# Three FFN blocks of a one-core decoder layer with six seven-product steps instead of five, another order of the low parts in runs of three, and the copies for premade weight sums on SyncE's queue

## The chip, the cores and the metric

One core of a Trainium2 chip runs one launch of the kernel. The metric is device time in microseconds (us), the median of three runs. The profile is one further execution of the same program.

## The reference

One trunk layer of a decoder, for 256 tokens, width 2048, all in float32. What matters here is how much of it is matrix products:

```
a = rmsnorm(h, norm_mix_pre);  proj = a @ w_in                     # 2048 x 17408
attn = three dilated-window attention groups;  r_out = gated linear recurrence (HGRN2)
y = sigmoid(gate_a) * (attn @ w_attn_branch) + sigmoid(gate_r) * (r_out @ w_hgrn_branch)
h = h + rmsnorm(y @ w_mix_out, norm_mix_post)                      # 2048 x 2048
a = rmsnorm(h, norm_ffn_pre)
gt, up = split(a @ w_ffn_gate_up)                                  # 2048 x 11264
h = h + rmsnorm((silu(gt) * up) @ w_ffn_down, norm_ffn_post)       # 5632 x 2048
```

The change lies in the product with `w_ffn_gate_up`.

## The kernel before

**High and low parts.** TensorE multiplies in a rounded float32 format. Each operand is therefore split: the high part is a rounded copy that ScalarE makes, the low part is what VectorE finds by subtracting the copy from the operand. A product is then three matmuls, high x high, high x low and low x high (`prod`, which calls `mm`, L171). For a weight tile of 128x2048 these parts are `w` (L399, ScalarE) and `wl` (L407, VectorE).

**Wide blocks and steps.** The gate and up columns are worked off in eleven blocks of 512 gate and 512 up columns. Block 0 is done in another way; blocks j = 1 to 10 are `Wide` blocks. Such a block has eight steps. A step takes two of the sixteen 128-row slices of the weights, for both column groups (gate, up) and both sides (the first and the last 128 tokens): a 2x2x2 product of tiles. Done plainly that is eight products, 24 matmuls. By Strassen and Winograd's scheme it is seven products, 21 matmuls, if sums are at hand: sums of activation tiles (`h7`, made once for each pair of slices by `pair_sums`, kept for all blocks) and three sums of weight tiles (`sum`, 128x1536, made for each step anew). These sums are split too: `dh` (L427, ScalarE) and `dl` (L430, VectorE). There is one buffer for `dh` and one for `dl`, so `dh` of one step can't be written before the last matmul that reads `dh` of the seven-product step before it.

**Which steps are by seven.** The strings of `FFN` tell it: "87877877" for j = 2 to 10 means that steps 1, 3, 4, 6 and 7 are by seven products. `order` gives the pairs of slices 0 to 4 to the sevens and 5 to 7 to the eights, so `h7` is needed for five pairs (`H7`).

**The order within a step.** In `multiply_wide` a seven-product step is a string of products. The letters o, u, 1 and 7 read `w` and `wl`; t, 6 and 5 read `dh` and `dl`. The letter x is the transposition of the finished block before, which is put into step 1. The order depends on the neighbours: "ou1x6t57" in step 1, "t65ou17" where a seven follows, "ou17t65" where one came before, "1765out" in a last step after a seven. After the last step `gather` takes the products 1, 6, 5 and 7 out of their banks (L534 on ScalarE, L536 to L539 on VectorE), and `add_up` adds the rest (L552).

**Premade sums.** Three VectorE additions make the sums of a step (`add_weights`, L415 to L417). For the steps in `READY` they are made long before by DMA in a DRAM tile: `sums_before` issues three copies (L458) and, some steps later, three accumulating DMAs (L462), all from GpSimd's queue (POOL). `get_ready` loads the result (L439, SyncE's queue, SP). In blocks 2 to 10 steps 1 and 3 have such sums; 4, 6 and 7 don't. `READY_IN` lists the units of the program in which `sums_before` goes a little further.

**What sets the order.** It is written out by hand. For each step n, `ahead(n)` issues what later steps need: the split of step n+2 (`split_wide`: high part, then its sums if they aren't premade, then the low part), the split of the sums of step n+1 (`split_sums`, in `st.rest`), and, in `load_behind`, the weight load that the freed buffer allows. Where steps n and n+1 are both by seven (`close`), the split of the sums is put off until the matmuls of step n are issued (`later`). Weight loads go through SP's queue; for a seven-product step an accumulating DMA from POOL's queue (L308) adds one slice to another in the loaded tile. Three `raw` buffers and a fourth hold loaded weights.

Of the kernel before, what the change touches and what calls it, by code (L numbers as in the profile page):

```python
# [32 lines left out]
COL_QR, COL_FR, COL_IR, COL_GR = 9216, 10240, 11264, 12288  # L33
COL_GA, COL_GB = 13312, 15360

X7, H7 = tuple(range(5)), tuple(range(5))
MIX = [[(3, 0), (4, 0), (5, 0), (0, 1), (6, 0), (1, 1), (2, 0), (7, 0)],
       [(3, 0), (4, 0), (0, 1), (5, 0), (1, 1), (2, 0), (6, 0), (7, 0)]]

# [4 lines left out]


EARLY = [order(x) for x in ["88878878", "87878787"] + ["87877877"] * 6 + ["88787787", "88787878"]]
FFN = [order(x) for x in ["88878787"] + ["87877877", "87877877", "87877877", "87877877", "87877877", "87877877", "87877877", "87877877", "87877877"]]
# [9 lines left out]
BESIDE, LAG = (2, 3, 4, 5, 6, 7), 22  # L57
WIDE_FQ, FLIP = 2, 1
KEPT_P, KEPT, KEPT_H = (18,), (6, 10), (16,)
READY, PACE, READY_IN, READY_TWICE = {(2, 1), (2, 3), (3, 1), (3, 3), (4, 1), (4, 3), (5, 1), (5, 3), (6, 1), (6, 3), (7, 1), (7, 3), (8, 1), (8, 3), (9, 1), (9, 3), (10, 1), (10, 3), (11, 6), (11, 10), (11, 14), (12, 4), (12, 8), (12, 12), (12, 16)}, (4, 6), ((-5, 0), (2, 110)), ((2, 64),)  # L60


class Block:
# [48 lines left out]
def tile_hybrid_block(ctx: ExitStack, tc: tile.TileContext, t, out):  # L112
    nc = tc.nc
# [333 lines left out]
    def sums_before(steps):  # L447

        def one(st):
            b = st.block  # L450
            m = b.order[st.i][0]
            t00, t01, t10, t11 = (
                b.w[(2 * m + k) * P : (2 * m + k + 1) * P, c : c + 512] for k in range(2) for c in b.cols
            )
            st.ready = dram.tile([P, 1536], F32, name=nm("ready"))
            mid, row, all4 = (st.ready[:, n * 512 : (n + 1) * 512] for n in range(3))
            for dst, src in (row, t00), (mid, t10), (all4, t11):
                nc.gpsimd.dma_start(dst, src)  # L458
            for dst, src in (row, t01), (mid, row), (all4, mid):
                for _ in range(PACE[0]):  # L460
                    yield
                nc.gpsimd.dma_start(dst, src, accum_op=OP.add)  # L462

        going = []
        while steps or going:
            if steps and (len(going) < 1 or all(g[1] >= PACE[1] for g in going)):
                going.append([one(steps.pop(0)), 0])
            for g in list(going):
                g[1] += 1
                if next(g[0], "end") == "end":  # L470
                    going.remove(g)
            yield

    def multiply_wide(st, sides=(0, 1), groups=(0, 1)):
# [1002 lines left out]
    def second_norm():  # L1477
        ss, s2 = small("ss"), small("s2")
        yield
        for n in range(8):  # L1480
            j, b = n // 2, n % 2
            nc.scalar.activation(
                ptile("junk"), h_t[j][:, b, :], AF.Square,
                accum_out=ss[:, 4 * b + j : 4 * b + j + 1],
            )
            if n < 4 or b == 1:
                yield
        add_parts(s2[:, :2], ss)
        rsqrt_mean(r2c, s2[:, :2], D)
        ready.add("r2")  # L1490
        if len(H7) > 4:
            for n in range(len(H7) - 2):
                kept["h", n] = dram.tile([P, 1024], F32, name=nm("kept"))
                nc.gpsimd.dma_start(kept["h", n], h_t[n].rearrange("p b c -> p (b c)"))

    def more_sums():
        for n in range(len(H7) - 2):
            h_t.pop(n)
        slot = lambda: hslot("so").rearrange("p b c -> p (b c)").bitcast(F32R)
        lanes[1].append(pair_sums(hT[0], H7[4:], h7, slot))  # L1500

    def h_back():
        for n in range(len(H7) - 2):
            h_t[n] = hslot("h")
            nc.gpsimd.dma_start(h_t[n].rearrange("p b c -> p (b c)"), kept["h", n])

# [281 lines left out]
    def ahead(n):  # L1788
# [22 lines left out]
        def rest():  # L1811
            next(parts, None)
# [17 lines left out]
    for n, st in enumerate(seq):  # L1830
# [118 lines left out]
```

## Time and profile before

| what | value |
|---|---|
| median of three runs | 1676.74 us (1676.22 to 1677.0) |
| the profiled execution's own time | 1675.0 us |
| its span, first to last instruction | 1673.2 us |
| granted TensorE clock, mean | 0.999 |
| busy: PE (matmul) / DVE (VectorE) / ACT (ScalarE) / POOL (GpSimd) | 1661.8 / 1477.7 / 960.5 / 230.4 us |
| matmuls | 8028 |
| chain that ended last | 93% PE, 3% DVE, 2% DMA |

Times in the profile are us from the span's start. PEld is TensorE's weight load, which overlaps the matmuls. A row of the timeline gives start, length, engine, source line, operation and `out<-in`; in brackets stands idle time just before and what ended it. Matmuls are pipelined, so a matmul that is shown with 0.39 us is followed by the next one earlier than that: the distance of the starts is what it costs.

The FFN blocks stand in the trace one behind the other, 41.1 us each: block 1 begins at about 1025 us, block 2 at 1066, block 4 at 1148, block 5 at 1189, block 10 at 1395; the down projection begins at 1436.

### The profile page before, as it was taken

The page shows a single profiled execution, that of the slowest core. Times are in us where ns is not written, and L with a number is a line of the kernel's source. Part 1 is how long each engine was busy: PE and PEld are TensorE (multiplying, and loading weights), DVE is VectorE, ACT ScalarE, POOL GpSimd, SP SyncE. Part 2 cuts the span into 40 slices and gives each one's busy share as a digit, 9 for nine tenths or more (in the row PEclk, how much of TensorE's full clock was granted, in tenths as well). Part 3 has the DMA queues.
Part 4 walks back from the last instruction along what each step waited for, and adds up shares of the span by engine and source line. Part 5 has one row for each costly group of instructions (what it writes and reads, how often), then busy time and mean ns, then how long its engine had stood idle before and what let it go on. Part 6 is the DMA issues. An engine that isn't in the chain of part 4 may idle for free.

```text
span 1673.2 us, 21505 instructions
## 1 busy us (share of the span) xinstructions
PE 1661.8 (99%) x8028; PEld 1390.4 (83%) x8028; DVE 1477.7 (88%) x1512; ACT 960.5 (57%) x959; POOL 230.4 (14%) x309
## 2 busy tenths in 40 slices
PE   9999999999999999999999999999999999999997
PEld 7888888888888888888888888888888888888886
DVE  6799999999987998867668888999999999899988
ACT  6566555565665444445445565666666666666664
POOL 0001111111003311313311010111111111000100
PEclk9999999999999999999999999999999999999999
DMA  8888888998769997969988857998988989887892
GB/s 283 268 261 258 269 244 264 277 289 274 234 204 316 313 268 219 279 209 303 297 249 250 279 187 245 274 277 273 282 280 268 283 268 278 255 256 236 258 307 103
DMA packets 235705, 436.56 MB, mean 261 GB/s; under 512 B 15408, under 2 KB 65632, under 8 KB 235600
## 3 DMA queue, kind: packets, MB, share of 16 engines
q1 hardware_dynamic: 195920, 345.94, 61.3%
q0 software_dynamic: 37056, 83.32, 22.7%
q10 hardware_dynamic: 2624, 5.92, 1.0%
q8 instruction: 63, 1.03, 0.3%
q14 instruction: 42, 0.34, 0.1%
HBM read 422.01 MB, written 52.43 MB: 284 GB/s over the span
## 4 chain that ended last, share of the span: by engine, by line
PE 93%; DVE 3%; DMA 2%; issue 1%; ACT 1%; SPq 0%; DVEq 0%; POOLq 0%; ACTq 0%
PE acc L171 52%; PE aux L171 39%; DMA raw<-in_w_mix_out 2%; DVE wl L407 1%; PE aux L1033 0%; DMA x<-in_x 0%; ACT w L399 0%; DVE dl L430 0%; PE acc L1534 0%; DVE fz L1666 0%; PE aux L651 0%; PE aux L1534 0%; DVE w L361 0%; ACT junk L1621 0%; ACT dh L427 0%
## 5 line engine op out<-in xcount | busy, mean ns | idle before, releaser
L399 ACT ACTIVATE w<-raw 128x2048 fp32r<-128x2048 f32 x220 | 420.8, 1914 | 228.3 <-PE acc L171 62.0
L407 DVE TENSOR_TENSOR wl<-raw,w 128x2048 fp32r<-128x2048 f32 x220 | 500.8, 2286 | 22.6 <-ACT w L399 21.1
L171 PE MATMUL acc<-xT,w 128*128 128x512 f32 (+1 forms) x1536 | 279.0, 339 | 0.0
L171 PEld LDWEIGHTS acc<-xT,w 128*128 128x128 f32 x1536 | 234.6, 188 | 33.3 <-DVE w L361 0.2
L360 ACT ACTIVATE w<-raw 128x1024 fp32r<-128x1024 f32 (+1 forms) x159 | 166.7, 1052 | 160.0 <-PE acc L171 107.6
L361 DVE TENSOR_TENSOR w<-raw,w 128x1024 fp32r<-128x1024 f32 (+1 forms) x159 | 193.1, 1216 | 66.7 <-ACT w L360 66.0
L427 ACT ACTIVATE dh<-sum 128x1536 fp32r<-128x1536 f32 x113 | 168.5, 1491 | 141.5 <-PE acc L171 59.4
L430 DVE TENSOR_TENSOR dl<-sum,dh 128x1536 fp32r<-128x1536 f32 x113 | 198.0, 1752 | 16.7 <-ACT dh L427 16.3
L171 PE MATMUL aux<-w,xT 128*128 128x512 f32 x534 | 174.1, 389 | 0.0
L171 PE MATMUL acc<-w,hT 128*128 128x512 f32 x504 | 152.9, 391 | 0.0
L171 PE MATMUL acc<-w,xT 128*128 128x512 f32 x422 | 125.4, 393 | 0.3 <-DVE w L361 0.2
L171 PE MATMUL aux<-w,hT 128*128 128x512 f32 x368 | 122.9, 390 | 0.0
L171 PEld LDWEIGHTS aux<-w,xT 128*128 128x128 f32 x534 | 100.2, 188 | 20.6
L171 PEld LDWEIGHTS acc<-w,hT 128*128 128x128 f32 x504 | 94.0, 188 | 19.8 <-DVE w L361 0.4
L171 PE MATMUL aux<-wl,xT 128*128 128x512 f32 x267 | 103.9, 389 | 0.0
L308 POOL DMA_DIRECT2D raw<-in_w_ffn_gate_up x48 | 42.3, 881 | 377.0 <-DMA raw<-in_w_ffn_gate_up 144.9
L171 PE MATMUL acc<-dh,so 128*128 128x512 f32 x260 | 92.9, 391 | 0.0
L171 PEld LDWEIGHTS acc<-w,xT 128*128 128x128 f32 x422 | 78.3, 188 | 17.4 <-DVE w L361 1.2
L308 POOL DMA_DIRECT2D raw<-in_w_in x43 | 37.9, 882 | 395.3 <-DMA raw<-in_w_in 243.9
L171 PE MATMUL aux<-w,a 128*128 128x512 f32 x260 | 83.3, 389 | 0.0
L171 PE MATMUL aux<-w,so 128*128 128x512 f32 x210 | 81.8, 389 | 0.0
L171 PE MATMUL acc<-w,so 128*128 128x512 f32 x210 | 81.8, 389 | 0.0
(340 smaller groups left out, 3018.7 us busy)
## 6 DMA issues: line engine op xcount, KB each, us to landing
raw<-in_w_in SPq DMA_DIRECT2D x271, 512.0 KB, 6.1
raw<-in_w_ffn_gate_up SPq DMA_DIRECT2D x176, 512.0 KB, 4.8
raw<-in_w_ffn_down SPq DMA_DIRECT2D x88, 512.0 KB, 5.5
sum<-ready SPq DMA_DIRECT2D x25, 768.0 KB, 6.8
ready<-in_w_ffn_gate_up POOLq DMA_DIRECT2D x72, 256.0 KB, 7.3
raw<-in_w_mix_out SPq DMA_DIRECT2D x32, 512.0 KB, 6.7
ready<-ready POOLq DMA_DIRECT2D x50, 256.0 KB, 7.1
raw<-in_w_ffn_gate_up POOLq DMA_DIRECT2D x48, 256.0 KB, 6.0
```

Source lines behind the costliest of these rows:

```text
L171: nc.tensor.matmul(ps, lhsT, rhs, start=start, stop=stop, skip_group_check=True)
L308: nc.gpsimd.dma_start(raw[:, :512], rows, accum_op=OP.add)
L360: nc.scalar.activation(wh[:, k], raw[:, k], AF.Copy)
L361: nc.vector.tensor_sub(wl[:, k], raw[:, k], wh[:, k].bitcast(F32))
L399: nc.scalar.activation(hi, raw, AF.Copy)
L407: nc.vector.tensor_sub(lo, raw, hi.bitcast(F32))
L427: nc.scalar.activation(hi, flat, AF.Copy)
L430: nc.vector.tensor_sub(lo, flat, hi.bitcast(F32))
```

## The change

In blocks 4, 7 and 10 the string becomes "87778777": steps 1, 2, 3 and 5, 6, 7 are by seven products, steps 0 and 4 by eight. A sixth pair of slices needs sums of activations, so `H7` gets a sixth element, and `more_sums` makes it in blocks 1 and 2, in the buffer `more`. In those three blocks the premade sums are for steps 2, 6 and 7; step 1, which had premade sums, now has its sums added by VectorE. Altogether 28 steps have premade sums, before it was 25. `READY_IN` leaves out the units 52 to 67 (the mix projection), so part of the accumulating DMAs is issued later, some of them in FFN blocks 1 to 4.

There are new orders of products: "out6517" in the middle of a run of three, and "17ou65t" in a last step whose two predecessors are by seven. In `ahead`, where step n+2 needs VectorE's additions, these now stand before the low part of step n+1's sums, in all FFN blocks. Where the split of the sums was put off and step n+2 is by seven, the rest of step n+2's split and its load come after the matmuls. The three copies of each premade sum are issued from SP's queue; the accumulating DMAs stay on POOL's.

In the whole program PE issues 9 matmuls fewer. VectorE gets 3 more `dl` and one more set of pair sums (f, three s, `more`); ScalarE 3 more `dh` and one `more`; SP gets 84 copies and 3 more loads of sums; POOL loses its 75 copies and gets 12 accumulating DMAs more, 9 for sums and 3 for weights.

```
-X7, H7 = tuple(range(5)), tuple(range(5))
+X7, H7, H_KEPT = tuple(range(5)), tuple(range(6)), 3
...
+SIX = (4, 7, 10)
+FFN = [order(x) for x in ["88878787"] + ["87778777" if j in SIX else "87877877" for j in range(2, 11)]]
...
-READY, PACE, READY_IN, READY_TWICE = {(2, 1), (2, 3), ... (12, 16)}, (4, 6), ((-5, 0), (2, 110)), ((2, 64),)
+READY = {(j, i) for j in range(2, 11) for i in ((2, 6, 7) if j in SIX else (1, 3))}
+READY |= {(11, 6), (11, 10), (11, 14), (12, 4), (12, 8), (12, 12), (12, 16)}
+PACE, READY_IN, READY_TWICE = (4, 6), ((-5, 0), (2, 52), (68, 110)), ((2, 64),)
...
             for dst, src in (row, t00), (mid, t10), (all4, t11):
-                nc.gpsimd.dma_start(dst, src)
+                nc.sync.dma_start(dst, src)
...
         elif st.last:
-            steps = "1765out" if seven[0] else "1657out"
+            steps = ("17ou65t" if b.order[i - 2][1] else "1765out") if seven[0] else "1657out"
         elif st.between:
             go["x"] = st.between() or (lambda: None)
             steps = "ou1x6t57"
         elif seven[0]:
-            steps = "ou17t65"
+            steps = "out6517" if seven[1] else "ou17t65"
...
     def more_sums():
-        for n in range(len(H7) - 2):
+        for n in range(H_KEPT):
             h_t.pop(n)
         slot = lambda: hslot("so").rearrange("p b c -> p (b c)").bitcast(F32R)
-        lanes[1].append(pair_sums(hT[0], H7[4:], h7, slot))
+        lanes[1].append(pair_sums(hT[0], H7[4:5], h7, slot))
+        lanes[1].append(pair_sums(hT[0], H7[5:], h7, lambda: p3("more", F32R, 1024, 1)))
...
+        if n + AHEAD >= len(seq):
+            if sums and not close:
+                next(sums, None)
+            return lambda: None
+        wide = type(st.block) is Wide
+        first = sums and not close and wide and st.block.stage == "ffn" and st.sums is None
+        if first:
+            next(parts, None)
         if sums and not close:
             next(sums, None)
-        if n + AHEAD >= len(seq):
-            return lambda: None
-        if type(st.block) is Wide:
+        if not wide:
+            split(st)
+        elif not first:
             next(parts, None)
-        else:
-            split(st)
...
-            if not late:
+            behind = later and seq[n + AHEAD].rest
+            if not late and not behind:
                 rest()
...
             flush(later)
             later.clear()
+            if behind:
+                rest()
```

The lines of the changed kernel stand 3 (in `multiply_wide` and before it) or more further down: L407 is L410 there, L430 is L433.

**First place, PE, block 4, from step 1 to step 2.** `w` and `wl` are a step's weights, `dh` and `dl` its split sums, `hT` and `so` activations and their sums. Before, the end of product 5 and product 7 of step 1, and the beginning of step 2 by eight products, of which 17 more matmuls follow:

```order
L171 MATMUL aux_9523<-dh_9447,so_8325 128x512
L171 MATMUL aux_9523<-w_9411,so_8325 128x512
L171 MATMUL aux_9523<-wl_9412,so_8325 128x512
L171 MATMUL aux_9523<-w_9411,so_8325 128x512
L171 MATMUL acc_9462<-w_9450,hT_7986 128x512
L171 MATMUL acc_9462<-wl_9451,hT_7986 128x512
L171 MATMUL acc_9462<-w_9450,hT_7986 128x512 x2
```

In the changed kernel, the same place, where step 2 is by seven in the order "out6517":

```order
L174 MATMUL aux_9555<-dh_9480,so_8329 128x512
L174 MATMUL aux_9555<-w_9439,so_8329 128x512
L174 MATMUL aux_9555<-wl_9440,so_8329 128x512
L174 MATMUL aux_9555<-w_9439,so_8329 128x512
L174 MATMUL acc_9495<-w_9483,hT_7984 128x512
L174 MATMUL acc_9495<-wl_9484,hT_7984 128x512
L174 MATMUL acc_9495<-w_9483,hT_7984 128x512
L174 MATMUL acc_9495<-w_9483,so_8414 128x512
L174 MATMUL acc_9495<-wl_9484,so_8414 128x512
L174 MATMUL acc_9495<-w_9483,so_8414 128x512
L174 MATMUL acc_9508<-dh_9562,hT_7984 128x512
L174 MATMUL acc_9508<-dl_9563,hT_7984 128x512
```

Between the last matmul that reads step 1's `dh` and the first that reads the next `dh` stood 3 + 24 matmuls; now 3 + 6 stand there.

On VectorE (DVE) at the same place, before: the low part of step 1's sums, `wl` of steps 2 and 3, `dl` of step 3, and the additions for step 4.

```order
L430 TENSOR_TENSOR dl_9448<-sum_1415_9341,dh_9447 128x1536
L407 TENSOR_TENSOR wl_9451<-raw_9310,w_9450 128x2048
L407 TENSOR_TENSOR wl_9489<-raw_9348,w_9488 128x2048
L430 TENSOR_TENSOR dl_9531<-sum_9409,dh_9530 128x1536
L415 TENSOR_TENSOR sum_1446_9537<-raw_9380 128x512
L416 TENSOR_TENSOR sum_1446_9537<-sum_1446_9537,raw_9380 128x512
L417 TENSOR_TENSOR sum_1446_9537<-sum_1446_9537,raw_9380 128x512
L407 TENSOR_TENSOR wl_9534<-raw_9380,w_9533 128x2048
```

And now: `dl` of step 1, `wl` of step 2, the additions for step 3, `dl` of step 2, `wl` of steps 3 and 4, `dl` of step 3.

```order
L433 TENSOR_TENSOR dl_9481<-sum_1431_9442,dh_9480 128x1536
L410 TENSOR_TENSOR wl_9484<-raw_9340,w_9483 128x2048
L418 TENSOR_TENSOR sum_1443_9524<-raw_9377 128x512
L419 TENSOR_TENSOR sum_1443_9524<-sum_1443_9524,raw_9377 128x512
L420 TENSOR_TENSOR sum_1443_9524<-sum_1443_9524,raw_9377 128x512
L433 TENSOR_TENSOR dl_9563<-sum_9437,dh_9562 128x1536
L410 TENSOR_TENSOR wl_9522<-raw_9377,w_9521 128x2048
L410 TENSOR_TENSOR wl_9572<-raw_9409,w_9571 128x2048
L433 TENSOR_TENSOR dl_9600<-sum_1443_9524,dh_9599 128x1536
```

The additions for step 3 have come ahead of step 2's `dl`. Not shown: the additions for step 1 now stand on VectorE ahead of `gather` of block 3.

**Second place, PE, end of block 4.** Before, the last step from product 6 on, in the order "1765out": 6, 5, o, u, and behind them t and the next block.

```order
L171 MATMUL aux_9504<-dh_9705,so_8735 128x512
L171 MATMUL aux_9504<-dl_9706,so_8735 128x512
L171 MATMUL aux_9504<-dh_9705,so_8735 128x512
L171 MATMUL aux_9523<-dh_9705,so_8735 128x512
L171 MATMUL aux_9523<-dl_9706,so_8735 128x512
L171 MATMUL aux_9523<-dh_9705,so_8735 128x512
L171 MATMUL acc_9462<-w_9637,hT_7984 128x512
L171 MATMUL acc_9462<-wl_9638,hT_7984 128x512
L171 MATMUL acc_9462<-w_9637,hT_7984 128x512
L171 MATMUL acc_9462<-w_9637,so_8735 128x512
L171 MATMUL acc_9462<-wl_9638,so_8735 128x512
L171 MATMUL acc_9462<-w_9637,so_8735 128x512
```

Now, the last step from product 6 on, in the order "17ou65t" (6, 5, t), and the first matmul of block 5:

```order
L174 MATMUL aux_9536<-dh_9739,more_8910 128x512
L174 MATMUL aux_9536<-dl_9740,more_8910 128x512
L174 MATMUL aux_9536<-dh_9739,more_8910 128x512
L174 MATMUL aux_9555<-dh_9739,more_8910 128x512
L174 MATMUL aux_9555<-dl_9740,more_8910 128x512
L174 MATMUL aux_9555<-dh_9739,more_8910 128x512
L174 MATMUL acc_9508<-dh_9739,hT_7988 128x512
L174 MATMUL acc_9508<-dl_9740,hT_7988 128x512
L174 MATMUL acc_9508<-dh_9739,hT_7988 128x512
L174 MATMUL aux_9796<-w_9710,hT_7988 128x512
```

Behind product 6 stood twelve matmuls of the block; now six stand there.

**Third place, DVE, block 2, steps 1 to 3.** Before: `dl` of step 1, `wl` of steps 2 and 3, `dl` of step 3, the additions for step 4.

```order
L430 TENSOR_TENSOR dl_8848<-sum_1317_8703,dh_8847 128x1536
L407 TENSOR_TENSOR wl_8851<-raw_8706,w_8850 128x2048
L407 TENSOR_TENSOR wl_8889<-raw_8747,w_8888 128x2048
L430 TENSOR_TENSOR dl_8931<-sum_8780,dh_8930 128x1536
L415 TENSOR_TENSOR sum_1354_8937<-raw_8783 128x512
L416 TENSOR_TENSOR sum_1354_8937<-sum_1354_8937,raw_8783 128x512
L417 TENSOR_TENSOR sum_1354_8937<-sum_1354_8937,raw_8783 128x512
L407 TENSOR_TENSOR wl_8934<-raw_8783,w_8933 128x2048
```

Now, with the first part of the sixth pair sums (f, s), and the additions ahead of `dl` of step 3:

```order
L433 TENSOR_TENSOR dl_8868<-sum_1320_8722,dh_8867 128x1536
L410 TENSOR_TENSOR wl_8871<-raw_8725,w_8870 128x2048
L578 TENSOR_TENSOR f_8908<-hT_7988 128x512
L565 TENSOR_TENSOR s_8911<-f_8908 128x256
L566 TENSOR_TENSOR s_8911<-s_8911,f_8908 128x128
L567 TENSOR_TENSOR s_8911<-f_8908,s_8911 128x128
L410 TENSOR_TENSOR wl_8917<-raw_8767,w_8916 128x2048
L418 TENSOR_TENSOR sum_1360_8965<-raw_8803 128x512
L419 TENSOR_TENSOR sum_1360_8965<-sum_1360_8965,raw_8803 128x512
L420 TENSOR_TENSOR sum_1360_8965<-sum_1360_8965,raw_8803 128x512
L433 TENSOR_TENSOR dl_8960<-sum_8800,dh_8959 128x1536
L410 TENSOR_TENSOR wl_8963<-raw_8803,w_8962 128x2048
```

Four pair-sum instructions and three additions have come ahead of step 3's `dl`.

More of the change, by code (lines that the diff above doesn't have):

```diff
@@ L46 @@
 EARLY = [order(x) for x in ["88878878", "87878787"] + ["87877877"] * 6 + ["88787787", "88787878"]]
-FFN = [order(x) for x in ["88878787"] + ["87877877", "87877877", "87877877", "87877877", "87877877", "87877877", "87877877", "87877877", "87877877"]]
+SIX = (4, 7, 10)
+FFN = [order(x) for x in ["88878787"] + ["87778777" if j in SIX else "87877877" for j in range(2, 11)]]
 DOWN = [[((n + 16 * j) % 22, n in by7) for n in range(KF // 2)] for j, by7 in enumerate( ([4, 6, 8, 10, 12, 14, 16, 18], [0, 2, 4, 6, 8, 10, 12, 14, 16, 18]))]
@@ L59 @@
 KEPT_P, KEPT, KEPT_H = (18,), (6, 10), (16,)
-READY, PACE, READY_IN, READY_TWICE = {(2, 1), (2, 3), (3, 1), (3, 3), (4, 1), (4, 3), (5, 1), (5, 3), (6, 1), (6, 3), (7, 1), (7, 3), (8, 1), (8, 3), (9, 1), (9, 3), (10, 1), (10, 3), (11, 6), (11, 10), (11, 14), (12, 4), (12, 8), (12, 12), (12, 16)}, (4, 6), ((-5, 0), (2, 110)), ((2, 64),)
+READY = {(j, i) for j in range(2, 11) for i in ((2, 6, 7) if j in SIX else (1, 3))}
+READY |= {(11, 6), (11, 10), (11, 14), (12, 4), (12, 8), (12, 12), (12, 16)}
+PACE, READY_IN, READY_TWICE = (4, 6), ((-5, 0), (2, 52), (68, 110)), ((2, 64),)
 class Block:
@@ L1496, in more_sums @@
     def more_sums():
-        for n in range(len(H7) - 2):
+        for n in range(H_KEPT):
             h_t.pop(n)
         slot = lambda: hslot("so").rearrange("p b c -> p (b c)").bitcast(F32R)
-        lanes[1].append(pair_sums(hT[0], H7[4:], h7, slot))
+        lanes[1].append(pair_sums(hT[0], H7[4:5], h7, slot))
+        lanes[1].append(pair_sums(hT[0], H7[5:], h7, lambda: p3("more", F32R, 1024, 1)))
     def h_back():
-        for n in range(len(H7) - 2):
+        for n in range(H_KEPT):
             h_t[n] = hslot("h")
```

## The prediction

> **What bounds the kernel now.** I read the page's busy times first.
>
> ```profile
> PE 1661.8 (99%) x8028; PEld 1390.4 (83%) x8028; DVE 1477.7 (88%) x1512; ACT 960.5 (57%) x959; POOL 230.4 (14%) x309
> ```
>
> PE is idle for 1673.2 - 1661.8 = 11.4 us of the span. The view by stretches says where, and how close VectorE runs in the stretches concerned (us, then busy time and instructions of PE, PEld, DVE, ACT, POOL, granted clock, DMA share, GB/s):
>
> ```profile
> 0.00:44.70 44.70, 42.77 (x196) 32.46 (x197) 29.12 (x56) 30.78 (x59) 1.07 (x9) 1.00 0.81 277
> 530.00:800.00 270.00, 269.63 (x1672) 238.65 (x1671) 226.34 (x340) 125.00 (x208) 75.55 (x109) 1.00 0.92 268
> 1107.20:1148.31 41.11, 41.11 (x187) 33.98 (x186) 37.91 (x30) 25.32 (x17) 4.39 (x5) 1.00 0.90 279
> 1148.31:1189.40 41.09, 41.09 (x187) 33.98 (x186) 37.86 (x30) 25.34 (x17) 4.41 (x5) 1.00 0.91 273
> 1660.00:1673.20 13.20, 4.60 (x21) 3.47 (x19) 9.34 (x20) 2.13 (x6) 0.00 (x0) 0.87 0.44 159
> ```
>
> The start (1.9 us) and the tail (8.6 us) hold nearly all the idle time, and the change touches neither. All else that PE could win from waits is 11.4 - 10.5 = 0.9 us. In an FFN block PE is full, and DVE is busy for 37.9 of 41.1 us: 3.2 us free. So PE sets the time, and DVE is the engine that can come to set it. The price of a matmul is the distance of starts, from the chain of waits (start, length, what):
>
> ```profile
> 1436.58 21.76 PE aux L171 x96
> ```
>
> 21.76 / 96 = 0.227 us.
>
> **What is saved.** Nine matmuls go: 9 x 0.227 = 2.04 us, 0.12%. A measurement of this kernel tells about 0.2% (3.4 us) from no change, so even the whole gain would read as the same. What decides is whether the new order makes PE wait.
>
> **What VectorE gets.** Groups of the whole run, shapes apart (busy us, mean ns of one, idle before):
>
> ```profile
> L407 DVE TENSOR_TENSOR wl<-raw,w 128x2048 fp32r<-128x2048 f32 x220 | 500.8, 2286 | 22.6 <-ACT w L399 21.1
> L430 DVE TENSOR_TENSOR dl<-sum,dh 128x1536 fp32r<-128x1536 f32 x113 | 198.0, 1752 | 16.7 <-ACT dh L427 16.3
> L427 ACT ACTIVATE dh<-sum 128x1536 fp32r<-128x1536 f32 x113 | 168.5, 1491 | 141.5 <-PE acc L171 59.4 <-PE aux L171 39.5 <-DVE sum L420 27.3
> ```
>
> A changed block has three steps with additions, as before, and one `dl` more: 37.9 + 1.75 = 39.6 us of DVE against 41.1 - 0.68 = 40.4 us of PE. On the average that fits, with 0.8 us free instead of 3.2; the order of the queues decides the rest.
>
> **First wait: `dh` and `dl` between steps 1 and 2 of blocks 4, 7 and 10.** The single `dh` must be read out, rewritten by ACT, and followed by `dl` on DVE. Block 2 of the profile has the same step 1 and shows the pieces:
>
> ```profile
> 1072.27 1.75 DVE L430 TENSOR_TENSOR dl<-sum,dh 128x1536 fp32r<-128x1536 f32 x1
> 1073.94 4.49 DVE L407 TENSOR_TENSOR wl<-raw,w 128x2048 fp32r<-128x2048 f32 x2
> 1076.12 0.40 PE L171 MATMUL aux<-dh,so 128*128 128x512 f32 x1
> 1076.60 1.50 ACT L427 ACTIVATE dh<-sum 128x1536 fp32r<-128x1536 f32 x1 [1.12 <-PE aux L171]
> 1078.35 1.75 DVE L430 TENSOR_TENSOR dl<-sum,dh 128x1536 fp32r<-128x1536 f32 x1
> 1080.01 0.68 DVE L415 TENSOR_TENSOR sum<-raw 128x512 f32<-128x512 f32 x1
> 1081.94 2.28 DVE L407 TENSOR_TENSOR wl<-raw,w 128x2048 fp32r<-128x2048 f32 x1
> 1082.73 0.39 PE L171 MATMUL acc<-dl,hT 128*128 128x512 f32 x1
> ```
>
> The last matmul on `dh` starts at 1076.12; `dh` of the next such step starts 0.48 later and ends at 1078.10. If `dl` began 0.03 behind it, it would end at 1079.88. Today it is wanted at 1082.73, so the way is hidden. After the change the matmul that wants it is the eleventh behind the one at 1076.12 (three of 7, six of o and u, then the first of t, on `dh`, and its second, on `dl`): 1076.12 + 11 x 0.227 = 1078.61. How long a waiting matmul takes to start once `dl` is there, and that such a wait exists at all, another place shows:
>
> ```profile
> 1431.31 1.75 DVE L430 TENSOR_TENSOR dl<-sum,dh 128x1536 fp32r<-128x1536 f32 x1
> 1433.12 0.50 PE L171 MATMUL aux<-dl,so 128*128 128x512 f32 x1 [0.24 <-DVE dl L430]
> ```
>
> 1433.12 - 1433.06 = 0.06. So PE would go on at 1079.94 instead of 1078.61: 1.3 us lost, whatever else DVE does. DVE makes it worse. Behind `dl` of step 1 it now does one `wl` (2.20 from start to start, half of 1073.94 to 1078.35), three additions (1080.01 to 1081.94: 1.93), then `dl`: 1073.94 + 4.13 = 1078.07, no later than `dh`. But step 1 has lost its premade sums, and its 1.93 us of additions stand ahead of `gather`, where DVE idles 1.52 us in today's blocks (the row is below); 0.4 us stay, and push everything behind. `dl` then starts at 1078.5, and the loss is 1.7 us. Bounds 1.2 and 1.9; I take 1.7, three times: 5.1 us. Nothing covers it: behind the waiting matmul stands all of PE, and for PE wait ACT's next `dh` and SP's next load.
>
> **Second wait: the end of blocks 4, 7 and 10.** `gather` begins when product 6 is read out; behind `gather` and `add_up` stands `wl` of the next block's step 1. End of block 4 and beginning of 5, before:
>
> ```profile
> 1186.29 0.62 PE L171 MATMUL aux<-dh,so 128*128 128x512 f32 x2
> 1186.71 0.60 ACT L534 ACTIVATE e<-aux 128x512 f32<-128x512 f32 x1
> 1187.35 0.69 DVE L536 TENSOR_TENSOR e<-aux,e 128x512 f32<-128x512 f32 x1 [1.52 <-ACT e L534]
> 1190.07 2.34 DVE L552 TENSOR_TENSOR e<-acc,e 128x1024 f32<-128x1024 f32 x2
> 1192.33 2.28 DVE L407 TENSOR_TENSOR wl<-raw,w 128x2048 fp32r<-128x2048 f32 x1
> 1194.90 0.39 PE L171 MATMUL aux<-wl,hT 128*128 128x512 f32 x1
> ```
>
> `wl` ends at 1194.61, the matmul that reads it starts at 1194.90: 0.29 us to spare. With "17ou65t" product 6 comes 6 matmuls nearer to the block's end, 6 x 0.227 = 1.36 us. The chain behind it is a chain on DVE without gaps, so 1.36 - 0.29 = 1.1 us are lost, part of it perhaps already in the next block's first matmul, whose bank `gather` has to free. Bounds 0.8 (should `wl` be put on the way sooner) and 1.3; 1.1, three times: 3.3 us. The `dl` of the last step is wanted 6 matmuls later in the new order, so the wait of 0.24 us shown above can go; I leave that out.
>
> **Third wait: step 3 of block 2.** Its `dl` ends at 1080.10 and is wanted at 1082.73: 2.6 us to spare. Ahead of it come the additions (1.93) and four pair-sum instructions, whose price block 1 shows from the first to what follows the fourth:
>
> ```profile
> 1051.28 0.68 DVE L575 TENSOR_TENSOR f<-hT 128x512 f32<-128x512 f32 x1
> 1052.99 0.68 DVE L419 TENSOR_TENSOR sum<-raw 128x512 f32<-128x512 f32 x1
> ```
>
> 1.71 + 1.93 - 2.57 = 1.1 us, bounds 0.5 and 1.3. In the blocks that keep their string the additions alone stand ahead of that `dl`, 1.93 of 2.6 us: no wait. Ahead of step 6 they fill DVE's wait for `dh` and cost nothing.
>
> **SP's queue.** 84 copies of 256 KB now stand between weight loads. Two kinds of DMA (count, size, median us from issue to landing), and the longest of ACT's waits between 530 and 700 us (total, times, longest):
>
> ```profile
> raw<-in_w_in SPq DMA_DIRECT2D x271, 512.0 KB, 6.1
> ready<-in_w_ffn_gate_up POOLq DMA_DIRECT2D x72, 256.0 KB, 7.3
> ...
> ACT w L360 <- PE acc L171: 57.8, 27, 3.5
> ```
>
> A group of three holds the queue for 768 KB / 268 GB/s = 2.9 us if nothing else moved. Between 530 and 800 us, where most groups lie, the DMA share is 0.92 and PE loses 0.37 us; ACT, which takes the loads first, waits there for PE to free its buffers, up to 3.5 us at a time, and for no load. So the loads have some us of lead, and that lead has to bear the delay. I take 0, bounds -0.5 (the mix projection, which has no such traffic now) and +5 (two late groups). POOL's 75 copies less are worth nothing: POOL is busy 14%.
>
> [...] No row of this profile has copies on SP's queue.
>
> **Sum.** -2.04 + 5.1 + 3.3 + 1.1 + 0 = +7.5 us. Span 1673.2 + 7.5 = 1680.7; that execution's own time 1675.0 + 7.5 = 1682.5; the median is 1.7 us above it, so 1676.7 + 7.5 = 1684.2 us, 0.45% slower.
>
> **Rivals.**
>
> *All waits hidden (not slower).* PE gains 2.04 us: 1674.7. It decides where ACT and DVE reach `dh` and `dl` in less than 2.5 us from the last reading matmul's start and DVE stays 1.4 us ahead at a block's end. For it: on the average DVE still has 0.8 us a block. Against it: 1.50 + 1.75 us are rows and exceed 2.5 by themselves. Chance 0.06.
>
> *One of the two repeated waits is absent.* Without the first: -2.04 + 3.3 + 1.1 = +2.4, 1679.1, the same. Without the second: -2.04 + 5.1 + 1.1 = +4.2, 1680.9. For it: 0.29 us of slack is a reading of one block. Chances 0.05 and 0.06.
>
> *Weight loads late on SP's queue.* The three waits and 3 to 6 us more: 1687 to 1690. For it the DMA share of 0.92, against it POOL's copies load the same engines today. Chance 0.14.
>
> *Faster by over 0.2%.* It needs the 2.04 us and more than the 0.9 us of other idle time; only a shift in the run would give it. Chance 0.03.
>
> **The numbers.** The forecast has 0.66, with its own range 1681 to 1686, about what all bounds at one end make (+4.0 and +8.9). Slower by over 0.2%: 0.66 + 0.06 + 0.14 = 0.86; the same: 0.06 + 0.05 = 0.11; faster 0.03. The range 1679.5 to 1688.5 takes in the forecast, the case without the second wait and the better half of the late loads.
>
> **What would show it.** 8019 matmuls show that the change does what it says. Right: PE waits for `dl` of 1.2 to 1.9 us some 12 us into blocks 4, 7 and 10, waits for `gather` or `wl` early in what follows them, and one for `dl` in block 2. Blocks 4 and 7 then take 41.1 - 0.7 + 1.7 = 42.1 us with 3 matmuls fewer, and blocks 5 and 8 take 42.2. Wrong: no PE wait in those stretches, or PE waits that go back to loads between 530 and 960 us.

## The result, and the profile after

The changed kernel takes 1693.31 us (median of 5 runs, 1690.99 to 1694.12), the kernel before 1676.74 in the same session (1675.70 to 1678.86). The ratio is 1.0101, 95% interval 1.009 to 1.0112: 16.6 us slower. The forecast said slower, 1684.2 us; its range ended at 1688.5.

The profiled execution of the changed kernel has a span of 1691.8 us at a granted clock of 0.999, against 1673.2 before. Of its page, the busy times, the bytes and the chain that ended last:

```profile
PE 1666.5 (99%) x8019; PEld 1386.6 (82%) x8019; DVE 1484.0 (88%) x1520; ACT 963.8 (57%) x963; POOL 199.5 (12%) x246
...
DMA packets 243961, 444.42 MB, mean 263 GB/s; under 512 B 15792, under 2 KB 66016, under 8 KB 243856
...
PE 74%; DVE 12%; DMA 8%; issue 4%; ACT 2%; SPq 0%; DVEq 0%; ACTq 0%; POOLq 0%
```

8019 matmuls: the nine are gone. DVE and ACT have hardly more work, but the chain now passes through DVE for 12% and through DMA for 8% of the span, 3% and 2% before. 7.9 MB more are moved. PE's waits (in all, times, longest):

```profile
PE acc L174 <- DVE dl L433: 4.9, 6, 1.3
PE aux L174 <- DVE dl L433: 4.3, 5, 1.3
PE aux L174 <- DVE wl L410: 3.2, 4, 1.1
PE acc L174 <- DVE wl L410: 2.3, 3, 0.9
```

Each of these rows ends with a low part that DVE has just written, as the forecast had it. What is behind DVE differs from place to place. By the starts of neighbouring matmuls in the trace, PE loses over the usual 0.227 us (a place has the time of the matmul ahead of the wait):

| place | us, each | sum | in the forecast |
|---|---|---|---|
| early wide blocks: 213, 365, 369, 429, 436 us | 1.01, 1.05, 1.00, 1.23, 0.70 | 5.0 | 0 |
| mix projection, 923 us (0.45 elsewhere gone) | 1.09 | 0.6 | 0 |
| start of the FFN: 1047, 1079 us | 1.25, 0.92 | 2.2 | 0 |
| block 2, `dl` of step 3 | 1.27 | 1.3 | 1.1 |
| blocks 4, 7, 10, `dl` of step 2 | 1.43, 1.41, 1.43 | 4.3 | 5.1 |
| end of blocks 4, 7, 10 (bank, then `wl`) | 0.94, 0.99, 0.98 | 2.9 | 3.3 |
| other `dl` in blocks 4 and 10 | 0.32, 0.70, 0.42 | 1.4 | 0 |

The first of the waits in block 4, from the timeline (start, length, engine, line, operation, out<-in; in brackets the idle time and what ended it):

```profile
1169.23 1.49 ACT L430 ACTIVATE dh<-sum 128x1536 fp32r<-128x1536 f32 x1 [1.10 <-PE aux L174]
...
1170.27 0.68 DVE L420 TENSOR_TENSOR sum<-sum,raw 128x512 f32<-128x512 f32 x1
...
1170.87 1.75 DVE L433 TENSOR_TENSOR dl<-sum,dh 128x1536 fp32r<-128x1536 f32 x1
1171.02 0.39 PE L174 MATMUL acc<-dh,hT 128*128 128x512 f32 x1
...
1172.67 0.50 PE L174 MATMUL acc<-dl,hT 128*128 128x512 f32 x1 [1.27 <-DVE dl L433]
1173.01 0.40 PE L174 MATMUL acc<-dh,hT 128*128 128x512 f32 x1
```

ACT starts `dh` only when PE has read the old one, `dl` follows 0.15 us behind its end, and PE stands. Note the 0.50 of the matmul that waited, and that the next starts 0.34 behind it: each wait costs 0.11 us more than its idle time.

The 21 waits less the one gone, with 0.11 us more each, and less the 2.04 us saved make 17.9 of the 18.6 us between the two spans.

What has to be explained are the 9 us of waits that no term of the forecast has, all but 1.4 of them ahead of block 2's step 3: whether they belong to the copies' queue, to the steps in which sums are now made, or to the six-step blocks.

### The profile page after: what moved, and what is told of

Same layout as the page of the kernel before. It is cut to its first block, busy times and chain, and to the rows that moved or that the text cites. A ratio compares the mean times of both kernels' runs of the same rounds, so it can differ in the third digit from the quotient of the medians.

```text
span 1691.8 us, 21566 instructions
## 1 busy us (share of the span) xinstructions
PE 1666.5 (99%) x8019; PEld 1386.6 (82%) x8019; DVE 1484.0 (88%) x1520; ACT 963.8 (57%) x963; POOL 199.5 (12%) x246
## 4 chain that ended last, share of the span: by engine, by line
PE 74%; DVE 12%; DMA 8%; issue 4%; ACT 2%; SPq 0%; DVEq 0%; ACTq 0%; POOLq 0%
PE acc L174 43%; PE aux L174 30%; DVE wl L410 4%; DMA raw<-in_w_ffn_gate_up 4%; DVE dl L433 2%; DMA raw<-in_w_in 2%; DMA raw<-in_w_mix_out 1%; ACT w L402 1%; DVE w L364 1%; PE aux L1036 0%; DVE e L555 0%; DMA raw<-in_w_ffn_down 0%; DVE sum L418 0%; DVE sum L420 0%; PE aux L654 0%
## 5 line engine op out<-in xcount | busy, mean ns | idle before, releaser
L410 DVE TENSOR_TENSOR wl<-raw,w 128x2048 fp32r<-128x2048 f32 x220 | 501.5, 2286 | 30.4 <-ACT w L402 29.0
L430 ACT ACTIVATE dh<-sum 128x1536 fp32r<-128x1536 f32 x116 | 172.9, 1490 | 149.5 <-PE acc L174 61.7
L433 DVE TENSOR_TENSOR dl<-sum,dh 128x1536 fp32r<-128x1536 f32 x116 | 203.3, 1752 | 20.5 <-ACT dh L430 20.0
L174 PE MATMUL acc<-w,hT 128*128 128x512 f32 x478 | 145.2, 391 | 0.0
L174 PE MATMUL acc<-w,xT 128*128 128x512 f32 x422 | 125.4, 393 | 0.3 <-DVE w L364 0.2
L174 PEld LDWEIGHTS acc<-w,hT 128*128 128x128 f32 x478 | 89.1, 188 | 19.2 <-DVE e L539 0.5
```

Source lines behind the costliest of these rows:

```text
L174: nc.tensor.matmul(ps, lhsT, rhs, start=start, stop=stop, skip_group_check=True)
L410: nc.vector.tensor_sub(lo, raw, hi.bitcast(F32))
L430: nc.scalar.activation(hi, flat, AF.Copy)
L433: nc.vector.tensor_sub(lo, flat, hi.bitcast(F32))
```

## Experiments

All ratios are to the kernel before, timed beside. "Groups" are the premade sums: three copies of 256 KB to DRAM, then three accumulating DMAs on POOL's queue. Before has 25 of them, the change 28.

### The queue of the copies, undone and alone

Undone in the changed kernel:

```diff
-                nc.sync.dma_start(dst, src)
+                nc.gpsimd.dma_start(dst, src)
```

> The changed kernel with the three copies of a premade sum back on POOL's queue, all else as changed. Theory A (the copies in SP's queue stand ahead of weight loads in the same queue, so that loads land late): the five waits of the early wide blocks (1.01, 1.05, 1.00, 1.23 and 0.70 us, 5.0 together) go, and with them perhaps those at 923, 1047 and 1079 us (0.64, 1.25 and 0.92): 1693.3 - 5.0 to 1693.3 - 7.8, so 1685.5 to 1688.3. Rival B (the waits at 923, 1047 and 1079 us come from accumulations that POOL now issues in other steps, by the numbers that say when sums are made ready): these three stay, 1688.3. Rival C (the queue of the copies is of no matter, the six-step blocks cost all of it): 1693 again.

Measured: 1691.24 us, ratio 1.0092 (1.0076 to 1.0107); the five runs lie far apart, 1687.51 to 1695.65, and the trace is of the longest. In it 1.8 us of the early waits are left, but as much comes back in other places up to block 2: 2.1 us at 946, 1.1 at 1029 and 1.95 at 1073. None of the three theories had that.

The opposite edit, in the kernel before:

```diff
-                nc.gpsimd.dma_start(dst, src)
+                nc.sync.dma_start(dst, src)
```

> The kernel before with nothing changed but the queue of the three copies, which becomes SP's. Theory A: waits like those at 213, 365, 369, 429 and 436 us of the changed kernel appear, 5 to 8 us in all: 1682 to 1685. Rival C: no wait that the kernel before lacks, 1676.7.

Measured: 1682.14 us, ratio 1.0040 (1.0028 to 1.0053), 6.7 us. The queue alone makes the waits at 214, 369, 429 and 437 us, and one of 0.8 at 1078. What is late there shows at the first group. The first weight load behind the point where the copies go out, in the kernel before, by its source line (count, duration of the issue in ns, start; then the time to landing):

```profile
L302 SPq DMA_DIRECT2D raw<-in_w_in x1: 384/384/384, 188.6 to 188.6; - x1
...
DMA to landing us min/median/max: 6.8/6.8/6.8
```

the copies there:

```profile
L458 POOL DMA_DIRECT2D ready<-in_w_ffn_gate_up x3: 862/893/908, 189.7 to 190.8; - x3
```

and with the copies on SP's queue, these copies and that load:

```profile
L458 SPq DMA_DIRECT2D ready<-in_w_ffn_gate_up x3: 591/716/1444, 186.2 to 187.6; - x3
```

```profile
L302 SPq DMA_DIRECT2D raw<-in_w_in x1: 390/390/390, 189.8 to 189.8; - x1
...
DMA to landing us min/median/max: 9.6/9.6/9.6
```

Before, POOL issued the copies at 189.7, behind this load; SP now issues them at 186.2, ahead of it. It is issued 1.2 us later, since the copies hold SP for 2.8, and takes 2.8 us more: landing at 199.4 instead of 195.4. The rest is the chain of waits of the same run (start, length, what):

```profile
200.06 4.98 DMA raw<-in_w_in
205.03 1.86 issue
206.89 0.70 DVE sum L419
...
213.24 1.76 DVE dl L430
215.01 0.04 issue
215.05 0.72 PE aux L171 x2
```

The DMA at 200.06 is POOL's accumulation into the landed tile, at 196.1 in the kernel before; DVE's sums, `dl` and PE follow, and PE loses 0.3 us at 211 and 1.0 at 214. The load that SP issued behind the copies landed 4.0 us later, with 768 KB of copies issued ahead of it. Whether the load stood behind them in SP's queue or only shared the DMA engines with them, these rows can't tell.

If order in SP's queue were all, another hardware queue would cure it:

```diff
-                nc.sync.dma_start(dst, src)
+                nc.scalar.dma_start(dst, src)
```

> The changed kernel with the three copies on ScalarE's queue, which carries no weight loads. If a copy delays what stands behind it in the same queue (theory A in its narrow form), the early waits go as with POOL's queue: 1685.5 to 1688.3, less whatever ScalarE loses by issuing 3 copies a group. If it is enough that the copies leave by a hardware queue at all and share the 16 engines with the loads, or that the sums are finished at another time, the waits stay: 1692 to 1694.

Measured: 1697.18 us, ratio 1.0128 (1.0113 to 1.0144). The wait at 213 is gone, but 1.59 and 1.02 us appear at 261 and 266, and 2.1 and 1.01 at 418 and 423. The load ahead of the wait at 261, which has no copies in its queue (issue, then landing; the kernel before has 6.1 us for it, issued at 239.9):

```profile
L305 SPq DMA_DIRECT2D raw<-in_w_in x1: 383/383/383, 239.8 to 239.8; - x1
...
DMA to landing us min/median/max: 11.4/11.4/11.4
```

ScalarE has issued three copies from 235.5 us on, which POOL issued from 247.2 on. So the narrow form of theory A falls: with copies that leave sooner a load with little lead takes longer to land, be they in its own queue (9.6 us instead of 6.8) or in another (11.4 instead of 6.1). That they take time on the DMA engines from it is a reading of these rows. Whether the place behind them in SP's queue adds to that, no run shows by itself.

### Three more groups, and the six-step blocks alone

With POOL's queue and the old steps for the sums, only the six-step blocks should be left:

```diff
-PACE, READY_IN, READY_TWICE = (4, 6), ((-5, 0), (2, 52), (68, 110)), ((2, 64),)
+PACE, READY_IN, READY_TWICE = (4, 6), ((-5, 0), (2, 110)), ((2, 64),)
...
-                nc.sync.dma_start(dst, src)
+                nc.gpsimd.dma_start(dst, src)
```

> The changed kernel with the copies on POOL's queue and with the numbers that say when sums are made ready as before: only the blocks with six steps by seven products, their orders and the sixth pair of sums are left of the change. If the forecast's three waits are right in kind, what is left is 4.27 us between steps 1 and 2 of blocks 4, 7 and 10, 2.91 at their ends and 1.27 in block 2, less 2.04 us of matmuls: 1676.7 + 6.4 = 1683.1. With the whole of the added time in the six-step blocks (rival C): 1693.

Measured: 1695.49 us, ratio 1.0120 (1.0106 to 1.0134). Far off, and not in blocks 4, 7 and 10: some 9 us go between 925 and 985. From 923 to 964 us 12 DMAs of groups start in this run, in the kernel before none. The six-step blocks bring three groups with them, and these now meet the loads of the mix projection, whose median to landing between 890 and 990 us is 9.9 us instead of 7.2. So they were left unmade, each such step reading the sums of the step before:

```diff
+            for k in SIX:
+                if st is made[k, 6]:
+                    made[k, 7].ready = st.ready
...
-    before = sums_before([
-        st for st in seq if type(st.block) is Wide and (blocks.index(st.block) - mix_last - 2, st.i) in READY
-    ])
+    before = sums_before([st for (j, i), st in made.items() if (j, i) not in [(k, 7) for k in SIX]])
```

(`made` holds the steps of READY by block and step.) Once with copies on POOL and the sums in the old steps, once with nothing else edited:

> The blocks with six steps by seven products alone, without what came with them: copies on POOL's queue, sums made in the same steps as before, and 25 groups of sums made as before instead of 28. Left out of the computation: the sums of the last step of blocks 4, 7 and 10 are not made; that step reads those of the step before it, with the same transfers, so its products are of no use. Theory D (the three more groups of premade sums, 18 transfers, cost what the run with 28 groups and POOL's queue lost between 925 and 985 us): nothing but the forecast's waits is left, 1675.4 + 4.3 + 2.9 + 1.2 - 2.0 = 1681.8, and no wait over 0.6 us before 1090 us. Rival (the six-step blocks alone cost the 16 to 20 us): 1692 to 1695.

> The changed kernel with 25 instead of 28 groups of sums made; copies on SP's queue as changed. Left out of the computation: as in the run above. With 6.7 us for the copies' queue (the run of the kernel before with SP's copies) and 6.4 for the forecast's waits, the three more groups are what is left of 16.6: 3.5 us. Theory D: 1689 to 1690, without the waits at 1047 and 1079 us. Rival: the queue and the six steps make each other worse and the groups cost nothing, 1693.

Measured: 1685.17 us, ratio 1.0054 (1.0041 to 1.0066), and 1689.03, ratio 1.0080 (1.0066 to 1.0094). The first, PE's waits:

```profile
PE acc L174 <- DVE dl L433: 3.4, 3, 1.3
PE aux L174 <- DVE dl L433: 2.4, 5, 1.3
PE aux L174 <- DVE wl L410: 1.2, 2, 0.6
...
PE acc L174 <- DVE wl L410: 0.6, 1, 0.6
```

This is the forecast's kernel, 9.4 us slower where 7.5 were forecast (its interval is 6.9 to 11.1 us), and no wait over 0.6 us ahead of block 2. The second lacks the waits at 1047 and 1079 us. Loads of `raw` between 1000 and 1090 us (count, size, median us to landing), in the changed kernel and then in this run:

```profile
raw<-in_w_ffn_gate_up SPq DMA_DIRECT2D x36, 512.0 KB, 7.2
```

```profile
raw<-in_w_ffn_gate_up SPq DMA_DIRECT2D x36, 512.0 KB, 4.9
```

The ledger: six-step blocks 9.4, copies on SP's queue with 25 groups 1689.0 - 1685.2 = 3.9, three more groups 16.6 - 13.3 = 3.3; together 16.6, as the last term is what is left. Each of these times is known to some 2 us by its interval, so the two smaller terms are known to about 3. They also depend on their order: with POOL's queue kept, the groups in the places of the change cost 15.8 - 9.4 = 6.4 us (the first run above), and SP's queue then 16.6 - 15.8 = 0.8. Only their sum, 7.2 us, doesn't depend on it.

Is it only the place? In the changed kernel's trace the last accumulation of a group goes out at 1090.6 us, in block 2; none is left for blocks 3 and 4. Groups may be made in blocks 3 to 5 instead:

```diff
-PACE, READY_IN, READY_TWICE = (4, 6), ((-5, 0), (2, 52), (68, 110)), ((2, 64),)
+PACE, READY_IN, READY_TWICE = (4, 6), ((-5, 0), (2, 52), (93, 140)), ((2, 64),)
```

> The changed kernel with copies on POOL's queue and the three last groups of sums made in blocks 3 to 5, not in the late mix projection (+9 us there) nor at the start of the FFN. All products are computed. If the three groups cost only by where they fall, as theory D has it: that of the six-step blocks alone, 1675.7 + 9.4 = 1685. If 18 more transfers cost wherever they are: 1688 to 1690.

> As the run above, but the copies of all groups except the first four on SP's queue: the change without the two costs that the forecast missed. 1685 + 0 to 1.8 us: 1685 to 1687. If SP's queue costs beyond the first four groups once the six-step blocks ask for loads: 1689.

> The changed kernel, copies on SP's queue, with nothing edited but the numbers that say where the last three groups of sums are made: blocks 3 to 5 instead of the start of the FFN. By the sums so far 1693.3 - 3.3 = 1690, without the waits at 1047 and 1079 us. Rival (those two waits come from copies or loads of other groups): 1692 to 1693.

Measured: 1694.99 us, ratio 1.0113 (1.0098 to 1.0128); 1694.88, 1.0116 (1.0102 to 1.0130); 1698.11, 1.0130 (1.0117 to 1.0144). Theory D falls as far as it promised a free place. In the third the waits at 1047 and 1079 us do go, so these were the three groups' work here, though the queue alone made one at 1078 in the kernel before; but block 4 then loses more. The chain in the first:

```profile
1168.31 10.10 DMA raw<-in_w_ffn_gate_up
...
1179.07 7.80 DMA raw<-in_w_ffn_gate_up
...
1188.76 1.48 ACT dh L430
```

A load and the accumulation on it take 18 us, and PE stands for 4.4 ahead of the first matmul that reads this `dh`. The three groups cost 3.3 us at the start of the FFN (6.4 with copies on POOL's queue), 18.2 - 9.4 = 8.8 in blocks 3 to 5, and 20.1 - 9.4 = 10.7 in the mix projection (the last two with copies on POOL's queue): nowhere tried were they free.

### Which copies cost

Before and after, the copies of the first four groups on POOL's queue and all others on SP's:

```diff
+            made.append(st)
+            q = nc.gpsimd if len(made) <= 4 else nc.sync
...
-                nc.sync.dma_start(dst, src)
+                q.dma_start(dst, src)
```

> The kernel before with the copies of all but the first four groups of sums on SP's queue. In the run with all copies there, the first load behind the first group's copies landed 3.9 us later than before, and what stood behind it had waits of 4.9 us up to 440 us, where only four groups fall; the 21 others cost 1.8. Theory A, placed: the loss hangs on those four groups, so 1675.7 + 1.8 = 1677.5, no wait over 0.6 us ahead of 440 us. Rival (the sums become ready at other times, or the hardware queue as such costs): about 1680 to 1682.

> The changed kernel with the copies of the first four groups of sums on POOL's queue, the other 24 on SP's. In the kernel before this edit took back the whole loss of the copies' queue. If the queue's cost is those four groups in the changed kernel too, the waits up to 440 us go and the rest stays: 1693.3 - 3.9 (the part measured with 25 groups) to - 5.0 (the waits in the trace), 1688 to 1689.5. Rival (whatever becomes earlier there is lost again in the late mix projection and at the start of the FFN, as with all copies on POOL's queue, where 2.2 us were late by 900 us and the end was as late as ever): 1691 to 1693.

Measured: the kernel before so edited 1675.87 us, ratio 1.0002 (0.9993 to 1.0011), and its waits are the old ones:

```profile
PE aux L171 <- DVE warm L213: 1.2, 1, 1.2
PE aux L171 <- DVE kk L1196: 0.4, 1, 0.4
PE aux L171 <- DVE dl L430: 0.2, 1, 0.2
PE acc L171 <- DVE w L361: 0.2, 1, 0.2
```

The changed kernel so edited takes 1688.26, ratio 1.0076 (1.0064 to 1.0089), 4.6 us less over before than unedited. In the kernel before, the four groups ahead of 440 us carry the whole cost of the queue; 21 others on SP's queue cost nothing. It also bears on the first run above: with all copies on POOL's queue the changed kernel is 15.8 us over before, with the first four there 12.0. By the medians the other 24 are better off on SP's queue, by 3.8 us; the intervals (1.0076 to 1.0107 and 1.0064 to 1.0089) overlap, so this is not shown.

### No six-step block, and the two repeated waits

```diff
-SIX = (4, 7, 10)
+SIX = ()
```

> The changed kernel with no block of six steps by seven: every FFN block has five again, 25 groups of sums, copies on SP's queue; the sixth pair of activation sums is still made. The waits in blocks 4, 7 and 10 and at their ends go, 2.0 us of matmuls come back, the wait in block 2 (1.27) stays: 1675.4 + 6.7 + 1.3 = 1683.4. If the early waits needed the six-step blocks too: under 1680.

Measured: 1680.97 us, ratio 1.0029 (1.0018 to 1.0039). No wait is left behind block 2's, which stays at 1.07. The early ones are there, 3.0 us. Less than expected by 2.4. Without block 2's wait 4.0 of the 5.2 us are left for the copies' queue and the places of the sums, near the 3.9 of the ledger and not the 6.7 that the expectation took from the kernel before.

The order of the last step's products, as before:

```diff
-            steps = ("17ou65t" if b.order[i - 2][1] else "1765out") if seven[0] else "1657out"
+            steps = "1765out" if seven[0] else "1657out"
```

> The changed kernel with the order of products of a block's last step as before (all seven products, then the outputs) in blocks 4, 7 and 10 too. The forecast's second wait is the distance of product 6 from the block's end: the waits at 1207, 1332 and 1459 us (0.76 each) and the ones ahead of the block's first matmul (0.20 each) go, 2.9 us. But the low part of the last step's sums is then wanted 6 matmuls (1.36 us) sooner, and 0.3 to 0.7 us of waits for it stand there already: 0.9 to 1.4 us each come back. Expected 1693.3 - 2.9 + 3.5 = 1694, 1690.5 if nothing comes back.

Measured: 1693.43 us, ratio 1.0103 (1.0089 to 1.0117), no change. The waits at the blocks' ends are gone, and in their place PE waits for the last step's `dl` by 1.14, 1.17 and 1.78 us; in block 4:

```profile
1199.72 0.50 PE L174 MATMUL aux<-dl,more 128*128 128x512 f32 x1 [0.98 <-DVE dl L433]
```

So the second wait is the order of the products, as forecast, and that order pays for another wait of its size.

Last, whether the first wait is the single buffer or DVE's three additions, which end 0.15 us behind `dh`:

```diff
-READY = {(j, i) for j in range(2, 11) for i in ((2, 6, 7) if j in SIX else (1, 3))}
+READY = {(j, i) for j in range(2, 11) for i in ((2, 3, 7) if j in SIX else (1, 3))}
```

> The changed kernel with the sums of step 3 of blocks 4, 7 and 10 made ahead and those of step 6 added up by DVE, where it was the other way round; as many of each. The three additions of step 3 stand on DVE directly ahead of the low part that the first wait is for, and end 0.15 us after the high part. If the one buffer of the high part sets the wait (last read, 0.47 us to ACT's start, 1.49 of ACT, 1.75 of DVE), it stays at 1.28 to 1.30 us instead of 1.42, three times. If DVE's additions set it, it shrinks by their 2.0 us and is gone. The additions of step 6 may cost a wait of their own ahead of steps 5 or 6: total 1692 to 1695 in the first case, 1689 in the second.

Measured: 1692.11 us, ratio 1.0100 (1.0085 to 1.0116); the three waits are 1.30, 1.29 and 1.30. DVE, then PE, in block 4:

```profile
1170.15 1.76 DVE L433 TENSOR_TENSOR dl<-sum,dh 128x1536 fp32r<-128x1536 f32 x1 [1.74 <-ACT dh L430]
```

```profile
1171.96 0.50 PE L174 MATMUL acc<-dl,hT 128*128 128x512 f32 x1 [1.14 <-DVE dl L433]
```

DVE now idles for 1.74 us ahead of `dl`, and PE waits all the same: it is the one buffer.

No run beats the kernel before; the best with all of the change's computation is the one at 1688.26. A second `dh` and `dl`, which should take the first wait away, were not tried.

## Why the prediction was wrong, point by point

**Its direction and its three waits were right.** "PE gains 2.04 us" holds, with 8019 matmuls. Taken with the 0.11 us that each wait adds on the matmul behind it (in the quoted row of the kernel before, the matmul at 1433.12 has the same 0.50), and in the run of the six-step blocks alone:

| step of the forecast | forecast | measured there |
|---|---|---|
| saved matmuls | -2.04 | -2.04 |
| first wait, three times | 5.1 | 3 x (1.42 + 0.11) = 4.6 |
| second wait, three times | 3.3 | 3 x (0.98 + 2 x 0.11) = 3.6 |
| third wait | 1.1 | 1.07 + 0.11 = 1.2 |
| sum | +7.5 | +7.3 |
| the run | | +9.4 |

That the sums agree so well is partly luck: the first wait was 0.5 too large, the second 0.3 too small. The first was oversized where the forecast added 0.4 us for additions on DVE: the turnaround alone is 1.3, as the last run shows, and DVE adds 0.12. What is missing to 9.4 are smaller waits without a term: 0.56 us at 418, 0.47 in block 3, 0.39 in block 7 and 0.15 in block 10, each with its 0.11, 2.0 in all. The forecast's "blocks 4 and 7 take 42.1 us" wasn't confirmed by itself; from the first wait in block 4 to that in block 7 (the row below, of the changed kernel) the three blocks take 1298.74 - 1172.67 = 126.1 us, where the forecast has 3 x 41.1 - 0.7 + 1.7 + 1.1 = 125.4.

```profile
1298.74 0.50 PE L174 MATMUL aux<-dl,hT 128*128 128x512 f32 x1 [1.25 <-DVE dl L433]
```

**The step that failed is "SP's queue", taken as 0.** It cost 6.7 us in the kernel before, 3.9 with the six-step blocks and 25 groups, and its first four groups 4.6 in the changed kernel: around the upper bound of 5. (With all copies of the changed kernel back on POOL's queue only 0.8 us came back, as the three more groups then cost 6.4 instead of 3.3.) The argument looked at 530 to 800 us, "where most groups lie", and found lead there. The runs show that it was right there (21 groups, no loss) and that nothing follows from it: four groups fall ahead of 440 us, where a load is followed by POOL's accumulation, DVE's sums and PE, with less to spare than the 4.0 us of the first group. The other three groups' loads were not followed. The sign that would prove it wrong, waits that go back to loads between 530 and 960, was put in the wrong place for the same reason. The rival "weight loads late on SP's queue", with 3 to 6 us and a chance of 0.14, is what happened in kind; its 1687 to 1690 still ends short of 1693.3, since it has no term for the three groups. That a group delays a load by its 2.9 us, of which one or two make the 3 to 6 us, no run shows; the runs showed 1.2 us until the first group's load was issued and 2.8 more until it landed. The reason it gave, the DMA share of 0.92 between 530 and 800 us, was not it: that is the stage that lost nothing. The objection to it, that POOL's copies load the same engines today, falls at the first group: they did so 3.5 us later, behind the load.

**A term was missing.** The prediction counted "84 copies" against 75 and costed only the queue of them. The nine more copies have nine more accumulations behind them, and that had to be done somewhere: 3.3 us in the place that the change gives it, by the run with 25 groups, in which the three more reads of sums stay. With these two, 7.5 + 3.9 + 3.3 = 14.7 of the 16.6 us; the 1.9 left are the difference of 9.4 and 7.5, which the smaller waits can make.

**The other rivals.** "All waits hidden" and "one of the two absent" are out by the traces; both repeated waits stand in blocks 4, 7 and 10.

## What to carry to other kernels

When DMAs move to another queue, ask for each stage which load they get ahead of and how much lead that load has; a mean DMA share, or the stage with the most of them, says nothing about the four that matter. When a table grows by three entries, follow all that one entry issues, and find the place on the DMA engines where it goes. And of a step with a single buffer, add up last read, rewrite and first use: here that gave 1.3 us to within 0.02.

## What the runs showed of the hardware

At a clock of 1.00 a matmul that had to wait showed 0.50 us instead of 0.39 and the next started 0.34 instead of 0.227 behind it, so that 20 more waits cost 2.2 us beside their idle time.

In three runs a long wait cost more than itself. In the run with 28 groups on POOL's queue in the old steps, PE idled for 1.43 and 1.82 us with one matmul between them:

```profile
949.38 0.50 PE L174 MATMUL aux<-w,yT 128*128 128x512 f32 x1 [1.43 <-ACT w L402]
951.71 0.79 PE L174 MATMUL aux<-wl,yT 128*128 128x512 f32 x1 [1.82 <-DVE wl L410]
952.30 0.63 PE L174 MATMUL aux<-w,yT 128*128 128x512 f32 x1
952.73 0.63 PE L174 MATMUL aux<-w,so 128*128 128x512 f32 x1
```

Behind them matmuls start 0.43 us apart, for 5 us. The windows of that stretch (length, busy us and count of PE, PEld, DVE, ACT and POOL, granted clock, DMA share, GB/s) have the clock at 0.66 there and at 1.00 ahead of it:

```profile
935.00:948.00 13.00, 12.29 (x53) 9.51 (x52) 7.03 (x9) 2.50 (x2) 1.81 (x2) 1.00 1.02 323
948.00:958.00 10.00, 6.79 (x17) 5.16 (x18) 9.47 (x8) 8.87 (x12) 4.24 (x6) 0.66 0.75 180
```

With the groups in blocks 3 to 5 and all copies on POOL's queue the same follows the wait of 4.4 us: matmuls 0.43 us apart from 1192.7 us on, and a clock of 0.72 between 1185 and 1197 us. It followed a shorter one too: in the first run of the experiments, with all copies of the changed kernel on POOL's queue, a single wait of 1.82 us, the one at 946, and a clock of 0.76 over the 7 us around it:

```profile
948.69 0.71 PE L174 MATMUL aux<-wl,yT 128*128 128x512 f32 x1 [1.82 <-DVE wl L410]
```

```profile
946.00:953.00 7.00, 5.13 (x15) 3.59 (x14) 6.52 (x5) 7.00 (x12) 0.57 (x1) 0.76 0.89 183
```

With the copies on ScalarE's queue, a wait of 1.83 us at 1033 leaves it at 1.00 (1032 to 1038 us), and so do the waits of the changed kernel, at most 1.3 us of idle time (1.00 between 1170 and 1177 us, around one of 1.27). So how long a wait may be isn't settled by its length alone, and what else settles it was not shown.

Issuing a DMA is not always cheap for SP: medians of 0.37 to 0.47 us for the weight loads of the kernel before, but 0.59, 0.72 and 1.44 for the three copies that the kernel before issues from SP's queue at 186 us when edited so, and the load behind them on SP's queue is issued at 189.8 us instead of 188.6.
